# Both feed-forward products of a hybrid encoder step as Strassen block products on one Trainium2 core

## The chip, the cores and the metric

The kernel runs on one core of a Trainium2 chip (trn2). The metric is device time in microseconds (us): how long one execution takes on that core. Engines are named as in the profile: PE is TensorE (matmuls; PEld its weight loads), DVE is VectorE, ACT is ScalarE, POOL is GpSimd, SP is SyncE, whose queue issues most DMAs.

## The reference

One step of a one-layer encoder for 512 prompt tokens and 64 sample tokens, 576 in all, with D_MODEL 2048 and D_FF 5632, in float32. The token mixer (sliding-window attention, a state-space branch, cross-attention into 256 memory tokens, three gates) comes first. The change concerns what follows it:

```
def conv_ffn(h, conv_prev, lp):
    t = h.shape[1]
    up = h @ lp['w_up']                       # 2048 -> 2 x 5632
    a, bv = jnp.split(up, 2, axis=-1)
    a_ext = jnp.concatenate([conv_prev.astype(a.dtype), a], axis=1)
    conv_w = lp['conv_w']
    a_conv = sum(a_ext[:, i:i + t] * conv_w[i] for i in range(CONV_W)) + lp['conv_b']
    out = (jax.nn.gelu(a_conv) * bv) @ lp['w_down']   # 5632 -> 2048
    return out, a_ext[:, -(CONV_W - 1):]

def layer(x, attn_past, s0, conv_prev, mem_k, mem_v, table, lp):
    ...
    x = x + rms_norm(mix, lp['norm_post_mix'])
    h2 = rms_norm(x, lp['norm_pre_ffn'])
    f, conv_new = conv_ffn(h2, conv_prev, lp)
    x = x + rms_norm(f, lp['norm_post_ffn'])
```

## The kernel before

**Layout.** Activations are kept transposed: channels on the 128 partitions, the 576 tokens along the row, in two halves of 288 (HT). A product's output row tile is 128 channels x 576 tokens in two PSUM banks.

**Three passes.** Float32 products are made of fp32r matmuls: each operand is split into a high part (rounded to fp32r) and a low part (what is left), and `gemm` (line 154) adds three products, high x high, high x low and low x high. A k-tile of 128 thus costs 3 passes x 2 halves = 6 matmuls of 288 columns per row tile, each with its own weight load.

**Weight stream.** The program is a list of blocks (`block`, line 91); a block is one weight tile of up to 128 x 1024 and a function that uses it. `go(i)` (line 1718) runs block i, and ahead of it issues the DMA of block i + 5 into one of four `raw` buffers (SP's queue, `dma_to`), makes the high part of block i + 2 on ScalarE (`h_to`, line 107, tile `wh`) and the low part of block i + 1 (of i + 2 for short blocks and at the end) on VectorE (`l_to`, line 118, tile `wl`); three buffers each. Each engine carries out its instructions in the order in which the program issues them; semaphores between the engines come from the tiles that they share.

**Side work** that isn't tied to a block is a list of generators (`side`); `side_step` advances one of them by a step between k-tiles.

**Feed-forward.** `up1_run` (line 1386) makes the first four row tiles of a k-tile by k-tile while x1, the residual after the mixer, is still being finished (`x1_next`); x1 also goes to DRAM (`x1d`). `ffn_open` then lays out the tiles of this phase, and `ffn_sums` and `ffn_rbc` make the norm's scale per token, which is applied to the outputs (`rbc`). Four tiles of the second half of w_up follow (`up_tile(i, 1)`), and for each further i a tile of each half: 40 x 2 tiles, each of 16 k-tiles in two blocks. `up_run` (line 1478) evicts a tile of the first half by a multiplication on VectorE (line 1497) and does the conv, GELU and scale (`conv`, line 1457: three VectorE instructions of 576 columns, one activation, one GpSimd multiplication at line 1475); a tile of the second half is multiplied with it (line 1503) and split into `gh` and `gl` (lines 1504, 1505), which stay on the chip. After every four of these tiles `down_run` (line 1517) takes their four k-tiles of w_down through all 16 output tiles, 8 blocks, and adds the result to `f` in SBUF (line 1529). The last four k-tiles are done by `last_run` (line 1532) in two parts of the tokens, with the second norm and residual behind each (`tail_*`). `x1tok` transposes x1 into token rows for that residual, as side work.

## Time and profile before

| | us |
|---|---|
| median of 3 runs | 3061.28 (3060.11 to 3063.08) |
| span of the profiled execution | 3060.8 |
| first matmul of the tail (line 1546) in that execution, from the span's start | 2978.34 |

The profiled execution has no other time beside its span; it lies 0.5 us below the median. The page gives the busy time of each engine, the span in slices, the chain of work that ended last, and the costliest groups of instructions, each with its line, what it writes and reads, the count, its busy time, the mean of one in ns and the idle time before. The 5504 x 3 matmuls on `xh` and `xl` at line 159 are those of the input and output projections and of up; the 1280 x 3 on `gh` and `gl` are down's. The blocks outside the feed-forward and the tail issue the same instructions after the change.

### The profile page before, as it was taken

How to read it: one execution, taken by the hardware profiler on the slowest of the kernel's cores; microseconds unless marked ns; L12 is line 12 of the kernel's file. 1: busy time of each engine (PE TensorE's matmuls, PEld its weight loads, DVE VectorE, ACT ScalarE, POOL GpSimd, SP SyncE). 2: the span in 40 equal slices, each digit the busy share in tenths (PEclk: the TensorE clock that was granted, in tenths of full speed). 3: DMA queues.
4: the chain of work that ended last, by engine and by line, in shares of the span. 5: the costliest groups of instructions: out<-in, count | busy, mean ns of one | idle time of the engine just before them, and what ended most of it. 6: DMA issues, size and time to landing. Idle time of an engine off the chain costs nothing.

```text
span 3060.8 us, 52554 instructions
## 1 busy us (share of the span) xinstructions
PE 3019.4 (99%) x22827; PEld 2964.2 (97%) x22827; DVE 1317.8 (43%) x2065; ACT 803.9 (26%) x1120; POOL 510.1 (17%) x548
## 2 busy tenths in 40 slices
PE   8999999999999999989999999999999999999997
PEld 7999999999999999979999999999999999999997
DVE  7334532444432243495444444434343434343447
ACT  4323332222222244452111212121212121212123
POOL 2200010133330024372020201010101010101015
PEclk9999999999999999999999999999999999999999
DMA  8622342334333345653333333222222222222235
GB/s 273 186 80 64 92 120 86 107 108 112 104 99 106 97 139 153 195 189 99 95 114 91 114 89 97 83 83 83 83 83 83 82 84 81 83 82 83 81 98 195
DMA packets 478630, 334.80 MB, mean 109 GB/s; under 512 B 57916, under 2 KB 447218, under 8 KB 477056
## 3 DMA queue, kind: packets, MB, share of 16 engines
q1 hardware_dynamic: 467344, 299.99, 33.1%
q0 software_dynamic: 6320, 21.99, 2.3%
q10 hardware_dynamic: 4736, 9.47, 0.8%
q8 instruction: 179, 2.93, 0.4%
q14 instruction: 51, 0.42, 0.0%
HBM read 293.22 MB, written 38.89 MB: 109 GB/s over the span
## 4 chain that ended last, share of the span: by engine, by line
PE 94%; DVE 3%; DMA 1%; POOL 1%; issue 1%; ACT 0%; DVEq 0%; ACTq 0%; POOLq 0%
PE ps L159 87%; PE ps L181 2%; PE ps L284 1%; DVE wl L118 1%; PE ps L1546 1%; DVE xl L1357 1%; DMA raw<-in_w_mem_kv_dram 0%; PE ps L1027 0%; PE ps L1031 0%; PE ps L579 0%; PE ps L613 0%; DMA raw<-in_w_out_dram 0%; PE ps L691 0%; POOL mixq L1347 0%; PE ps L662 0%
## 5 line engine op out<-in xcount | busy, mean ns | idle before, releaser
L159 PE MATMUL ps<-xh,wh 128*128 128x288 f32 x5504 | 1200.8, 298 | 3.1 <-DVE r_ss L1323 2.0
L159 PE MATMUL ps<-xh,wl 128*128 128x288 f32 x5504 | 1190.9, 296 | 7.6 <-DVE wl L118 7.6
L159 PE MATMUL ps<-xl,wh 128*128 128x288 f32 x5504 | 1189.6, 296 | 3.2 <-DVE xl L1357 3.2
L159 PEld LDWEIGHTS ps<-xh,wh 128*128 128x128 f32 x5504 | 889.0, 189 | 15.8 <-issue 9.9
L159 PEld LDWEIGHTS ps<-xh,wl 128*128 128x128 f32 x5504 | 890.6, 189 | 9.8 <-DVE wl L118 9.7
L159 PEld LDWEIGHTS ps<-xl,wh 128*128 128x128 f32 x5504 | 890.3, 189 | 4.7 <-DVE xl L1357 4.6
L107 ACT CAST wh<-raw 128x1024 fp32r<-128x1024 f32 (+2 forms) x478 | 482.1, 1009 | 992.3 <-PE ps L159 717.4
L118 DVE TENSOR_TENSOR wl<-raw,wh 128x1024 fp32r<-128x1024 f32 (+2 forms) x486 | 597.1, 1237 | 232.4 <-ACT wh L107 232.1
L159 PE MATMUL ps<-gh,wh 128*128 128x288 f32 x1280 | 274.2, 296 | 0.0
L159 PE MATMUL ps<-gl,wh 128*128 128x288 f32 x1280 | 274.1, 296 | 0.0
L159 PE MATMUL ps<-gh,wl 128*128 128x288 f32 x1280 | 274.0, 296 | 0.0
L1529 DVE TENSOR_TENSOR f<-ps,f 128x576 f32<-128x576 f32 x144 | 109.1, 758 | 243.5 <-PE ps L159 240.9
L159 PEld LDWEIGHTS ps<-gh,wl 128*128 128x128 f32 x1280 | 206.2, 189 | 0.0
L159 PEld LDWEIGHTS ps<-gl,wh 128*128 128x128 f32 x1280 | 206.2, 189 | 0.0
L159 PEld LDWEIGHTS ps<-gh,wh 128*128 128x128 f32 x1280 | 206.2, 189 | 0.0
L1461 POOL COPY cst<-mtmp 128x2 f32<-128x2 f32 x43 | 8.3, 193 | 1064.7 <-DVE mtmp L1497 1054.1
L1497 DVE TENSOR_TENSOR mtmp<-ps,rbc 128x576 f32<-128x576 f32 x40 | 30.3, 758 | 311.4 <-PE ps L159 311.4
L1503 DVE TENSOR_TENSOR c<-ps,c 128x576 f32<-128x576 f32 x44 | 33.3, 757 | 275.5 <-PE ps L159 269.8
L1474 ACT ACTIVATE c<-c,cvt 128x576 f32<-128x576 f32 x44 | 34.2, 778 | 390.9 <-DVE c L1473 390.9
L1143 ACT COPY ev<-ps 128x576 f32<-128x576 f32 x48 | 30.8, 642 | 272.9 <-PE ps L159 272.9
L1504 ACT CAST gh<-c 128x576 fp32r<-128x576 f32 x44 | 29.7, 674 | 271.4 <-DVE c L1503 271.4
L1475 POOL TENSOR_TENSOR c<-c,rbc 128x576 f32<-128x576 f32 x44 | 71.1, 1615 | 103.6 <-ACT c L1474 103.6
(407 smaller groups left out, 2009.7 us busy)
## 6 DMA issues: line engine op xcount, KB each, us to landing
raw<-in_w_up_dram SPq DMA_DIRECT2D x180, 512.0 KB
raw<-in_w_in_dram SPq DMA_DIRECT2D x118, 512.0 KB
raw<-in_w_down_dram SPq DMA_DIRECT2D x96, 512.0 KB
gd<-ev SPq DMA_DIRECT2D x48, 288.0 KB
gate<-gd SPq DMA_DIRECT2D x48, 288.0 KB
raw<-in_w_mem_kv_dram SPq DMA_DIRECT2D x16, 512.0 KB
raw<-in_w_out_dram SPq DMA_DIRECT2D x72, 96.0 KB
raw<-in_w_out_dram SPq DMA_DIRECT2D x18, 384.0 KB
```

Source lines behind the costliest of these rows:

```text
L107: (nc.vector.tensor_copy if 4 <= i < KD else nc.scalar.copy)(h[:, 0:n], raws[i][:, 0:n])
L118: E.tensor_tensor(out=lo[:, 0:n], in0=raw[:, 0:n], in1=hls[i][0][:, 0:n].bitcast(F32), op=ALU.subtract)
L159: mm(ps[:, a, 0:HT], w[:, c0:c0 + P], x[:, a * HT:(a + 1) * HT], start=start and i == 0, stop=stop and i == 2,)
L181: nc.tensor.transpose(out, in_, ident[0:k, 0:k])
L284: mm(mps[t][:, a, :], x[:, c], w[:, a * 512:(a + 1) * 512], start=k == 0 and i == 0, stop=k == KD - 1 and i == 2)
L1143: nc.scalar.copy(halves(e), ps[:, :, 0:HT])
L1357: nc.vector.scalar_tensor_tensor(out=xl[:, k, c], in0=x1[:, c], scalar=gcol[:, G_FFN, k:k + 1], in1=xh[:, k, c].bitcast(F32), op0=ALU.mult ...
L1474: nc.scalar.activation(c, c, AF.Gelu_apprx_tanh, bias=w(3))
L1475: nc.gpsimd.tensor_tensor(out=c, in0=c, in1=F["rbc"], op=ALU.mult)
L1503: nc.vector.tensor_tensor(out=halves(c), in0=ps[:, :, 0:HT], in1=halves(c), op=ALU.mult)
L1529: nc.vector.tensor_tensor(out=halves(f), in0=ps[j][:, :, 0:HT], in1=halves(f), op=ALU.add)
L1546: mm(ps[:, j, 0:n], w[:, c], x, start=k == 0 and i == 0, stop=k == 3 and i == 2)
```

## The change

Each pair of row tiles (up: A11, A12, A21, A22 are the two row tiles by the two halves of the k-tiles; down: two output tiles by k-tiles taken in twos) with the two halves of the tokens is a 2 x 2 block product. It is made in seven block products (Strassen's scheme in Winograd's order) in place of eight. Four of the seven weight operands of a group are sums that VectorE makes from weight tiles before they are split as any other (`s_to`); the activations' operands are made once:

- up: `xcombos` reads x1 back from DRAM k-tile by k-tile, makes the four combined operands on GpSimd and VectorE, splits them, and puts three of them into a new tile E; the fourth goes through DRAM (`x4d`) and, by `x4_load`, into the place of a plain operand that isn't needed any more. The first four tiles of each half of w_up stay as before.
- between: the conv's steps run as side work (`conv_pair`, `conv_steps`), its first multiplication on ScalarE, its scaling and the product with the second half on GpSimd. `gcombos` makes and splits the seven operands for down and stores them to DRAM (`gcd`), on ScalarE's queue (high parts) and GpSimd's (low parts).
- down: runs after all of up, in five chunks of 8 k-tiles (4 pairs), each chunk for 8 pairs of output tiles. `ring_load` brings a chunk's seven operands from DRAM through GpSimd's queue, the first chunk's one by one behind the products of the last up group, into two sets of slots in the space of xh, xl and E. The last 4 k-tiles stay plain (`last_run`, which takes its operands from the same slots).

A group's products go to three PSUM banks (A, C, A, B, A, C, A); a bank is copied out and added to again. x1's transposition (`xtok`) has its copies on ScalarE now. There are 3 `raw` buffers in the shared pool and one or two extra ones in a phase's own pool. In the diff's core, `stt` is a VectorE SCALAR_TENSOR_TENSOR, and context lines are cut.

```diff
+    def raw_tile(kind):
+        if extra["pool"] is not None and extra["kind"] == kind:
+            extra["turn"] = (extra["turn"] + 1) % (3 + extra["n"])
+            if extra["turn"] >= 3:
+                return extra["pool"].tile([P, 1024], F32, tag="rawx", name="raw", bufs=extra["n"])
+        return wp.tile([P, 1024], F32, tag="raw", name="raw", bufs=3)
...
+    def s_to(j):
+        while pos["s"] <= min(j, len(blocks) - 1):
+            i = pos["s"]
+            n, src = blocks[i][0], blocks[i][3]
+            raws[i] = src() if src else raws[i][:, 0:n]
+            pos["s"] += 1
...
+            lo = w_tile("wl", kind)
+            out, hi = as_src(raw, lo, n), as_src(raw, hls[i][0], n).bitcast(F32)
+            if kind == 2:
+                nc.vector.scalar_tensor_tensor(
+                    out=out, in0=raw, scalar=1.0, in1=hi, op0=ALU.mult, op1=ALU.subtract
+                )
+            else:
+                E = nc.gpsimd if i >= len(blocks) - 8 and i % 2 else nc.vector
+                E.tensor_tensor(out=out, in0=raw, in1=hi, op=ALU.subtract)
...
                 kk = kb * 2 + k
-                if kk == KD - 1:
-                    ffn_open()
                 x1_next()
...
+                if kk == KD - 1:
+                    ffn_open()
+                    for j in range(NG1):
                         (nc.vector.tensor_copy if j % 2 else nc.scalar.copy)(
-                            halves(F["a"][j][:, 2:2 + T]), ps[:, :, 0:HT])
+                            halves(F["a"][j][:, 2:2 + T]), F["ps"][j][:, :, 0:HT])
                         if j == 1:
                             ffn_sums()
...
+    def opnd(o, hl, s0, n=None):
+        x = (xh_t, xl_t)[hl][0]
+        ps = lambda k: k if n is None else slice(k, k + n)
+        if o in (0, 3):
+            return x[:, ps(s0), HT:T] if o else x[:, ps(s0), 0:HT]
+        if o in (1, 2):
+            return x[:, ps(8 + s0), 0:HT] if o == 1 else x[:, ps(8 + s0), HT:T]
+        return F["E"][:, hl, (2, 0, 1)[o - 4], ps(s0), :]
+    SEVEN = (0, 5, 4, 1, 6, 2, 3)
+    def product(bank, h, lo, j, n, s0, start, hook=None):
+        o = SEVEN[j]
+        for p in range(n):
+            xh, xl = opnd(o, 0, s0 + p), opnd(o, 1, s0 + p)
+            for i, (w, x) in enumerate(((h, xh), (h, xl), (lo, xh))):
+                mm(bank, w[:, p * P:(p + 1) * P], x, start=start and p == 0 and i == 0, stop=p == n - 1 and i == 2,
+                   skip_group_check=True)
+            if hook:
+                hook(p)
...
+    def stt(out, a, s, b, op):
+        nc.vector.scalar_tensor_tensor(out=out, in0=a, scalar=s, in1=b, op0=ALU.mult, op1=op)
+    def low(out, x, hi):
+        stt(out, x, 1.0, hi.bitcast(F32), ALU.subtract)
...
+    def xcombos():
+        E = F["E"]
+        G = nc.gpsimd
+        for p in range(8):
+            xa, xb = x_bufs(p)
+            a0, a1, b0, b1 = xa[:, 0:HT], xa[:, HT:T], xb[:, 0:HT], xb[:, HT:T]
+            for x, k in ((xa, p), (xb, p + 8)):
+                G.tensor_scalar(out=x, in0=x, scalar1=gcol[:, G_FFN, k:k + 1], scalar2=None, op0=ALU.mult)
+            G.tensor_tensor(out=a0, in0=a0, in1=a1, op=ALU.subtract)
+            G.tensor_tensor(out=a1, in0=b1, in1=a1, op=ALU.subtract)
+            yield
+            yield
+            yield
+            stt(b1, a0, -1.0, b1, ALU.subtract)
+            stt(b0, b1, -1.0, b0, ALU.subtract)
+            x2 = xa.rearrange("p (o c) -> p o c", o=2)
+            nc.scalar.copy(E[:, 0, 0:2, p, :], x2)
+            yield
+            nc.scalar.copy(E[:, 0, 2, p, :], b1)
+            gh = F["p"].tile([P, T], F32R, tag="gh", name="gh", bufs=2)
+            nc.scalar.copy(gh[:, 0:HT], b0)
+            low(E[:, 1, 0:2, p, :], x2, E[:, 0, 0:2, p, :])
+            nc.scalar.dma_start(x4d[0, :, p], gh[:, 0:HT].bitcast(F32))
+            yield
+            gl = F["p"].tile([P, T], F32R, tag="gl", name="gl")
+            low(E[:, 1, 2, p, :], b1, E[:, 0, 2, p, :])
+            low(gl[:, 0:HT], b0, gh[:, 0:HT])
+            nc.gpsimd.dma_start(x4d[1, :, p], gl[:, 0:HT].bitcast(F32))
+            if p + 2 < 8:
+                x_load(p + 2)
+    def x4_load():
+        for hl in range(2):
+            nc.gpsimd.dma_start(opnd(3, hl, 0, 8).bitcast(F32), x4d[hl])
...
+    def conv_steps(i, a):
         cv = cvt
         w = lambda j: cv[:, j, i:i + 1]
+        c = ev("c")
+        F["c", i] = c
+        e = F["p"].tile([P, 6], F32, tag="e", name="e", bufs=2)
+        nc.scalar.activation(c, a[:, 2:578], AF.Identity, scale=w(2))
+        nc.gpsimd.tensor_copy(e[:, 0:2], cv[:, 4:6, i])
+        nc.gpsimd.tensor_copy(e[:, 2:4], a[:, 514:516])
...
+        yield
...
-        V.tensor_scalar(out=c, in0=a[:, 2:578], scalar1=w(2), scalar2=None, op0=ALU.mult)
         V.scalar_tensor_tensor(out=c, in0=a[:, 1:577], scalar=w(1), in1=c, op0=ALU.mult, op1=ALU.add)
         V.scalar_tensor_tensor(out=c, in0=a[:, 0:576], scalar=w(0), in1=c, op0=ALU.mult, op1=ALU.add)
+        yield
...
+        yield
...
+    def scaled(a):
+        nc.gpsimd.tensor_tensor(out=a[:, 2:2 + T], in0=a[:, 2:2 + T], in1=F["rbc"], op=ALU.mult)
...
+    def conv_pair(q):
+        yield
+        yield
+        g0, g1 = (conv_steps(2 * q + m, F["a2"][m]) for m in range(2))
+        for g in (g0, g0, g0, g1, g0, g1, g0, g1, g1, g1):
+            next(g, None)
+            yield
...
+    def g_out(x, gh, ops, q, n=T):
+        gl = F["p"].tile([P, T], F32R, tag="gl", name="gl")
+        low(gl[:, 0:n], x[:, 0:n], gh[:, 0:n])
+        store(0, ops, q, gh)
+        store(1, ops, q, gl)
...
+    def gcombos(q):
+        c0, c1 = F.pop(("c", 2 * q)), F.pop(("c", 2 * q + 1))
+        plain = q >= NI // 2 - N_PLAIN
+        n = T if plain else HT
+        gh0 = g_hi(c0, n)
+        yield
...
+        a0, a1, b0, b1 = c0[:, 0:HT], c0[:, HT:T], c1[:, 0:HT], c1[:, HT:T]
+        nc.gpsimd.tensor_tensor(out=a0, in0=a0, in1=a1, op=ALU.subtract)
+        nc.gpsimd.tensor_tensor(out=a1, in0=b1, in1=a1, op=ALU.subtract)
+        for _ in range(3):
+            yield
+        g_out(c1, gh1, (1, 2), q)
+        yield
+        stt(b1, a0, -1.0, b1, ALU.subtract)
+        stt(b0, b1, -1.0, b0, ALU.subtract)
+        gh0 = g_hi(c0)
+        yield
+        gh1 = g_hi(c1)
+        yield
+        yield
+        g_out(c0, gh0, (5, 6), q)
+        for _ in range(4):
+            yield
+        g_out(c1, gh1, (3, 4), q)
...
+    def up2_run(i, kb):
...
+                side_step()
...
+                c = F["c", i]
+                nc.vector.tensor_tensor(out=halves(c), in0=ps[:, :, 0:HT], in1=halves(c), op=ALU.mult)
+                if i % 2 == 1:
+                    side.insert(0, gcombos(i // 2))
+            elif i == NG1 - 1:
+                side_drain()
+                x4_load()
...
+    def up_group(q, part):
+        R = {}
+        last = q == NI // 2 - 1 and part == 1
...
+                    F["sum"] = F["p"].tile([P, 4 * 578], F32, tag="sa", name="sums")
+                s = [F["sum"][:, 0:1024], F["sum"][:, 1024:2048]]
+                g = lambda x: s[x] if isinstance(x, int) else R[x]
+                stt(s[j], g(a), 1.0, g(b), ALU.add)
+                return s[j]
...
+        def run(j):
+            def run_(h, lo):
...
+                s1, s5, s2 = S["s"]
+                bank = (A, C, A, B, A, C, A)[j]
+                product(bank, h, lo, j, 8, 0, j in (0, 1, 3), lambda p: side_step() if p % 2 else None)
+                d0, d1 = F["a2"]
+                lo_, hi_ = slice(2, 2 + HT), slice(2 + HT, 2 + T)
+                if j == 0:
+                    nc.scalar.copy(s1, A)
+                elif j == 1:
+                    nc.scalar.copy(s5, C)
+                elif j == 2:
+                    nc.scalar.copy(s2, A)
+                elif j == 3:
+                    nc.vector.tensor_tensor(out=d0[:, lo_], in0=B, in1=s1, op=ALU.add)
+                elif j == 4:
+                    stt(d1[:, hi_], A, -1.0, s5, ALU.subtract)
+                elif j == 5:
+                    nc.vector.tensor_tensor(out=d0[:, hi_], in0=C, in1=s2, op=ALU.add)
+                    after(0)
                 else:
...
+                    nc.scalar.activation(d1[:, lo_], A, AF.Identity, scale=-1.0)
+                    after(1)
+                    if not part:
+                        side.append(conv_pair(q))
+                    elif not last:
+                        side.append(gcombos(q))
...
+                if last:
+                    ring_load(0, SEVEN[j])
...
+                    if j == 6:
+                        down_open()
...
+        def after(m):
+            a = F["a2"][m]
+            if not part:
+                scaled(a)
+                return
+            c = F["c", 2 * q + m]
+            E = nc.vector if last else nc.gpsimd
+            E.tensor_tensor(out=c, in0=c, in1=a[:, 2:2 + T], op=ALU.mult)
+        srcs = [lambda: R["A11"], add(0, "A21", "A22"), add(1, 0, "A11"), lambda: R["A12"],
+                add(0, "A11", "A21"), add(1, 1, "A12"), lambda: R["A22"]]
+        loads = [ld("A11", 0, 0), both, None, ld("A12", 0, 1), None, None, None]
+        for j in range(7):
+            block(1024, loads[j], run(j), srcs[j], 2)
...
+    def ring_load(c, o):
+        n = NP if c < NCH else N_PLAIN
+        for hl in range(2):
+            nc.gpsimd.dma_start(opnd(o, hl, 4 * (c % 2), n).bitcast(F32), gcd[hl, o, :, c * NP:c * NP + n, :])
...
+    def down_open():
+        side_drain()
+        for _ in gcombos(NI // 2 - 1):
+            pass
...
+        for o in SEVEN:
+            ring_load(1, o)
...
+    def down_group(c, mp):
...
+                    R["sum", j] = sum_tile(j)
...
+                nc.vector.tensor_tensor(out=o.rearrange("p (j c) -> p j c", j=NP), in0=v(a), in1=v(b), op=ALU.add)
...
+        srcs = [lambda: blk(0, 0), add(0, (1, 0), (1, 1), True), add(1, 0, (0, 0), True), lambda: blk(0, 1),
+                add(2, (0, 0), (1, 0), True), add(1, 1, (0, 1), False), lambda: blk(1, 1)]
...
+                bank = (A, C, A, B, A, C, A)[j]
+                product(bank, h, lo, j, NP, 4 * (c % 2), j in (0, 1, 3))
+                f0, f1 = F["f"][2 * mp], F["f"][2 * mp + 1]
+                f11, f12, f21, f22 = f0[:, 0:HT], f0[:, HT:T], f1[:, 0:HT], f1[:, HT:T]
+                dst = (f11, f22, f12, f11, f22, f12, f21)[j]
+                plus = j not in (1, 4, 6)
+                if c == 0 and j in (0, 1, 2, 6):
+                    nc.scalar.activation(dst, bank, AF.Identity, scale=1.0 if plus else -1.0)
+                else:
+                    nc.vector.tensor_tensor(out=dst, in0=dst, in1=bank, op=ALU.add if plus else ALU.subtract)
+                if mp == 0 and j == 6 and c >= 1:
+                    for o in SEVEN if c + 1 < NCH else (0, 3, 1, 2):
+                        ring_load(c + 1, o)
+            return run_
+        for j in range(7):
+            block(512, load if j == 0 else None, run(j), srcs[j], 3)
...
+        et = F["ep"].tile([P, 2 * 3 * 8 * HT], F32, tag="E", name="et")
+        F["ft"], F["grow"], F["acc"] = et[:, 0:10240], et[:, 10240:12288], et[:, 12288:12288 + T]
+        g = I["norm_post_ffn"]
+        nc.gpsimd.dma_start(F["grow"], bass.AP(g.tensor, g.offset, [[0, P], [1, D]]))
...
     def go(i):
-        dma_to(i + RAW_AHEAD)
-        h_to(i + 2)
-        l_to(i + (2 if N_SHORT <= i < LATE0 or i >= len(blocks) - 8 else 1))
+        if i < N_U2 + 8:
+            dma_to(i + RAW_AHEAD)
+            h_to(i + 2)
+            l_to(i + (2 if N_SHORT <= i < LATE0 else 1))
+        elif i < N_DOWN:
+            dma_to(min(i + 9, N_DOWN))
+            s_to(i + 3)
+            h_to(i + 2)
+            l_to(i + 2)
+        elif i < N_TAIL:
+            last = N_TAIL - 1 if i < N_TAIL - 2 else N_TAIL
+            dma_to(i + 8)
+            s_to(min(i + 4, last))
+            h_to(min(i + 3, last))
+            l_to(min(i + 3, last))
+        else:
+            dma_to(i + 4)
+            h_to(i + 2)
+            l_to(i + (2 if i >= len(blocks) - 8 else 1))
```

The blocks are listed in the order: the first four tiles of the first half of w_up, those of the second, the 40 groups of up, the 40 of down, the tail.

More of the change, by code (lines that the diff above doesn't have):

```diff
@@ L1430, in ffn_rbc @@
     def ffn_rbc():
-        ps = ps_rot()
+        ps = ps_side()
         bcast_cols(ps, F["y"])
@@ L1450, in ffn_open @@
-        F["cst"] = p.tile([P, 2, 2, NI], F32, name="cst")
-    def first_conv(j):
-        a = F["a"][j]
-        nc.vector.tensor_tensor(out=a[:, 2:2 + T], in0=a[:, 2:2 + T], in1=F["rbc"], op=ALU.mult)
-        conv(j, a)
-    def conv(i, a):
+        extra.update(pool=p, n=2, kind=2, turn=0)
+        F["xr"] = [p.tile([P, 1024], F32, tag="rawx", name="xc", bufs=2) for _ in range(2)]
+        sa = p.tile([P, 4 * 578], F32, tag="sa", name="a4")
+        F["a"] = [sa[:, j * 578:(j + 1) * 578] for j in range(4)]
@@ L1557, in run @@
                 l_to(cur["i"] + 2)
-            if a == 1 and mb == 0:
-                for hf in range(2):
-                    F["xs", hf] = wp.tile([P, 1024], F32, tag="raw", name="xs", bufs=4)
-                    nc.sync.dma_start(F["xs", hf][0:64], x1td[512:576, hf * 1024:(hf + 1) * 1024])
             if a == 1 and 1 <= mb <= 6:
```

358 lines of the change are left out of this document (224 added, 134 removed).

## The prediction

> **What bounds the kernel now.** I read the page first, then the chain that ended last in order of time, then the busy times of the feed-forward stretch, then the single instructions that the change multiplies. From the page:
>
> ```profile
> span 3060.8 us, 52554 instructions
> PE 3019.4 (99%) x22827; PEld 2964.2 (97%) x22827; DVE 1317.8 (43%) x2065; ACT 803.9 (26%) x1120; POOL 510.1 (17%) x548
> PE 94%; DVE 3%; DMA 1%; POOL 1%; issue 1%; ACT 0%; DVEq 0%; ACTq 0%; POOLq 0%
> ```
>
> TensorE is the chain. Busy time of pipelined matmuls doesn't say how fast they follow each other; the chain in order of time does (start, length, what):
>
> ```profile
> 1851.97 1126.40 PE ps L159 x8448
> 2985.81 3.52 PE ps L1546 x24
> ```
>
> 8448 matmuls of 288 columns without a break in 1126.40 us: 133.3 ns each. The second row is the tail, whose matmuls have 320 columns and go three times running into one PSUM bank: 146.7 ns each, that is 32 columns more at the same 13 ns over the columns at 2.4 per ns. So running into one bank costs nothing, and I price the new products, 24 or 12 matmuls into one bank, at 133.3 ns.
>
> The other engines in the same stretch (busy us of PE, weight load, DVE, ACT, POOL, then granted clock, DMA share, GB/s):
>
> ```profile
> 1600.00:2954.00 1354.00, 1354.00 (x10164) 1354.00 (x10164) 543.17 (x684) 263.81 (x280) 119.89 (x198) 1.00 0.29 86
> ```
>
> VectorE is busy 40%, ScalarE 19%, GpSimd 9%, DMA 29%. The room that the change must fit in is VectorE's other 60%.
>
> **What goes.** Up: 40 groups (20 pairs of row tiles in each half of w_up) take 2 x 96 matmuls each before, 7 products x 8 x 3 = 168 after: 7680 to 6720. Down: 10 chunks x 8 x 48 = 3840 to 5 x 8 x 7 x 4 x 3 = 3360. 1440 matmuls fewer at 133.3 ns: **-192.0 us**. The rest of the program's matmuls stay, the 80 transposes of x1 too; only their evictions move, from VectorE to ScalarE, which has the time (below).
>
> **What comes, on VectorE and GpSimd.** One instruction at a time: first VectorE, then GpSimd.
>
> ```profile
> 2007.17 0.76 DVE L1505 TENSOR_TENSOR gl<-c,gh 128x576 fp32r<-128x576 f32 x1 [0.74 <-ACT gh L1504]
> 2007.85 2.36 DVE L118 TENSOR_TENSOR wl<-raw,wh 128x1024 fp32r<-128x1024 f32 x2
> 2020.61 0.82 DVE L1470 SCALAR_TENSOR_TENSOR c<-mtmp,cvt,c 128x576 f32<-128x576 f32 x1
> 2021.86 0.22 DVE L1473 SCALAR_TENSOR_TENSOR c<-e,cvt 128x2 f32<-128x2 f32 x1
> 2022.00 1.22 DVE L118 TENSOR_TENSOR wl<-raw,wh 128x1024 fp32r<-128x1024 f32 x1
> L1265 DVE TENSOR_TENSOR gate<-ps,gate 128x288 f32<-128x288 f32 x8 | 3.6, 449 | 0.0
> L118 DVE TENSOR_TENSOR wl<-raw,wh 128x512 fp32r<-128x512 f32 x17 | 11.6, 681 | 0.0
> ```
>
> ```profile
> 1325.05 0.90 POOL L1348 TENSOR_TENSOR mixq<-mixq,xTr 128x288 f32<-128x288 f32 x1
> 1408.71 1.43 POOL L1475 TENSOR_TENSOR c<-c,rbc 128x576 f32<-128x576 f32 x1 [2.36 <-ACT c L1474]
> L1008 POOL MEMSET tz<- 128x1024 f32 x6 | 5.7, 956 | 33.3 <-PE ps L959 26.2 <-DMA tz<-kt 3.7 <-PE ps L1031 3.5
> ```
>
> A SCALAR_TENSOR_TENSOR is 0.06 us dearer than a TENSOR_TENSOR (0.82 against 0.76), so 1.28 for 1024 columns; an instruction behind another starts about 0.08 early (2.36 for two of 1.22), so 1.20 in a row, and in the same way 0.43 for 288 columns (0.82 less 288 columns at 1.03 ns, the slope between 0.76 and 1.22).
>
> Take a pair of up tiles, both halves of w_up, as the unit. TensorE: 336 x 133.3 = 44.8 us (51.2 before). VectorE: 14 low parts and 8 sums of 1024 columns, 22 x 1.20 = 26.4; two convs, each 2 x 0.82 + 3 x 0.22, with gaps 4.7; the combinations of the products' operands (gcombos), 3 of 288 and 3 of 576 columns, 3.7 with the 0.08 taken off; 6 evictions from PSUM at 0.45, 2.7. Together **37.5 us, 84%** of TensorE's 44.8. ScalarE, whose rows are
>
> ```profile
> L107 ACT CAST wh<-raw 128x1024 fp32r<-128x1024 f32 x410 | 429.5, 1047 | 903.4 <-PE ps L159 641.8 <-issue 222.3 <-ACT wh L107 27.5
> L1143 ACT COPY ev<-ps 128x576 f32<-128x576 f32 x48 | 30.8, 642 | 272.9 <-PE ps L159 272.9
> ```
>
> has 14 casts, 14.7 us, 8 small evictions of about 0.4 and some 8 others of 0.4 to 0.8: 24 us, half its time. It is hidden. So are the transfers: four weight tiles, 2.1 MB, per 22.4 us and 2.1 MB of stores per 44.8 us are 94 and 46 GB/s, on DMA engines that are busy 29% at 86; if they were late, each late weight tile would cost TensorE its delay, as the buffers hold five tiles.
>
> GpSimd gets 6 TENSOR_TENSOR of 576 columns and 2 of 288 per pair, 10.4 us, besides small copies and DMA issues. By itself that is nothing in 44.8. But the two engines shut each other out:
>
> ```profile
> 1553.02 0.80 POOL L1465 COPY e<-mtmp 128x2 f32<-128x2 f32 x1
> 1556.18 2.32 POOL L1475 TENSOR_TENSOR c<-c,rbc 128x576 f32<-128x576 f32 x1 [2.36 <-ACT c L1474]
> 1559.81 0.58 POOL L1600 DMA_DIRECT2D xr<-x1d  x1
> ```
>
> ```profile
> 1552.95 0.82 DVE L1469 SCALAR_TENSOR_TENSOR c<-mtmp,cvt,c 128x576 f32<-128x576 f32 x1
> 1553.81 0.82 DVE L1470 SCALAR_TENSOR_TENSOR c<-mtmp,cvt,c 128x576 f32<-128x576 f32 x1
> 1555.99 3.59 DVE L118 TENSOR_TENSOR wl<-raw,wh 128x1024 fp32r<-128x1024 f32 x2
> ```
>
> GpSimd's multiplication starts inside the first of two low parts and takes 2.32 instead of 1.43; the two low parts take 3.59 instead of 2.36. So VectorE pays 1.23 for one GpSimd multiplication of 576 columns, nearly all of it, and I put 0.7 for one of 288. It pays nothing for GpSimd's small copies (0.82 and 0.82 beside the 0.80). Per pair 6 x 1.23 + 2 x 0.7 = 8.8, so VectorE needs 37.5 + 8.8 = 46.3 if every one hits. Its PSUM evictions and two-column instructions (4.0 of the 37.5) can run beside GpSimd; that saves about a ninth of the 8.8, which leaves 45.3. Both stand above 44.8, and VectorE also waits for casts and products now and then, with two products (6.4 us) of lookahead to absorb it. I take **46.2 per pair, +1.4 over TensorE, x 20 = +28 us**. Ends: 0 (all of it absorbed) and 49.7 per pair (46.3 and another 3.4 us of waits in VectorE's order of work), +98.
>
> The Trainium skill says the same in "SBUF — State Buffer", section "SBUF: two separate sides": VectorE with two SBUF inputs and a GpSimd instruction that reads SBUF hold a shared port pair exclusively, for a whole instruction. It speaks against this change, which loads both; with whole instructions, 37.5 + 10.4 = 47.9, this term would be 62 us. The trace agrees in kind, with 1.23 of the 1.43 as the price.
>
> **Opening of the up products.** While the four remaining plain tiles run (384 matmuls, 51.2 us), xcombos builds the x operands. VectorE: 8 low parts at 1.14, 9.1; eight k-tile pairs of 4 x 0.43 + 0.74, 19.7; four convs 9.2; one gcombos 3.7; evictions and the rest 4: 45.7. GpSimd's shut-outs: 16 scalings of 576 columns, not in the trace, between 0.5 (the memset's rate, 956 ns for 1024) and 1.23: I take 0.7, 11; 18 of 288 at 0.7, 12.6; 8 of 576 at 1.23, 9.8: 33.4. Together 79, less some 4 beside PSUM work, against 51.2. VectorE runs in order, so its backlog holds the low parts behind it, and TensorE with them: **+24 us**. Ends 8 (scalings beside VectorE, lookahead used up) and 38 (1.23 each). The reload of the last of these operands (x4_load) waits on GpSimd's queue for their stores and for half of the fourth plain tile; behind it stand the first up group's scalings, which nobody wants for another 20 us. The eviction of the four accumulators now stands behind all of the last k-tile instead of between: +1.
>
> **Down.** A group is 84 matmuls, 11.2 us. VectorE: 11 of 512 columns at 0.60 in a row and 7 evictions at 0.45, 9.8 us; GpSimd only issues loads. That fits, 88%, with a bank's next product one product (1.6 us) away: 0. Without that cover, 0.1 us per product would be 28 us over 280.
>
> Its operands come from DRAM: 1.18 MB for each of seven, issued one product (3.2 us) apart in the last up group.
>
> ```profile
> q0 software_dynamic: 6320, 21.99, 2.3%
> ```
>
> 21.99 MB in 2.3% of the span are 312 GB/s; weights take 2.1 MB per 22.4 us, 94, which leaves 218 or 5.4 us an operand. Each load waits on GpSimd's queue for its product; what stands behind it there is the next load and the last stores, since the last group's multiplications are VectorE's. From that group's start the sixth lands at 35.6 and the seventh at 41.0, where the down products want them at 30.4 and 32.0. The weights pause when TensorE does: **+8 us**, ends 0 and 15. Later chunks have 90 us for 8.3 MB and stay hidden. The tail gets three weight buffers for four and loads its norm weights late: +3, ends 0 and 10.
>
> **Sum** against the profiled span, 3060.8, 0.5 below the median of the runs: 3060.8 - 192.0 + 28 + 24 + 1 + 8 + 3 = 2932.8; for the median **2933 us**.
>
> **Rivals.** First, the shut-out is absorbed: up pairs run at 44.8 and the opening at its low end: 3061.3 - 192 + 8 + 1 + 4 + 3 = 2885. For it: VectorE's 45.3 is only 1% over. Against: the opening needs half as much again as there is time for.
>
> Second, VectorE's order of work costs more than its sum: a conv step that waits for a late GpSimd product holds every low part behind it. At 49.7 per pair, 2933 + 70 = 3003. For it: GpSimd's 1.43 became 2.32 with VectorE busy 40%, and it is to be 84%.
>
> Third, slower than before: if all that GpSimd does at the port shuts VectorE out, its small copies (3.2 us per pair) and DMA issues (stores and row loads, about 10 of 0.6) too, a pair is 37.5 + 10.4 + 3.2 + 6 = 57.1, +12.3 x 20 = 246, so 3061.3 - 192 + 246 + 36 = 3151. It decides from (192 - 36) / 20 + 44.8 = 52.6 per pair. Against: the 0.82 beside the 0.80 copy. The box on DMAs from GpSimd's queue in the same section of the skill has descriptors starve while VectorE runs in a two-port mode; the only two-port work left here is small, and the row of 0.58 stands in a stretch in which VectorE was busy.
>
> That the change doesn't do what it says is no rival for the count: 1440 is fixed by the loops. For the pace it would be, and the 146.7 ns speak against it.
>
> **Chances.** Forecast (2905 to 2965) 0.54; absorbed (2875 to 2905) 0.17; order of work (2965 to 3050) 0.20; slower 0.08; no difference 0.01. The range of 2885 to 3000 takes the first whole, some 0.13 of the second and of the third each: 0.80. 0.2%, 6 us, is about what a measurement here tells from no change: faster 0.91, same 0.01, slower 0.08.
>
> **What would show it.** Right: 1440 fewer matmuls; a product of 24 at 3.2 us where nothing stalls; up pairs of some 46 us, TensorE waiting there for wl, and VectorE's 1024-column instructions with a mean well above 1.28; the longest waits between the plain tiles and the first up products; a short wait for DMA at the first down group, and down groups at 11.2. Wrong: up pairs at 44.8 (absorbed) or 49 (order of work), a down group over 11.2, or products slower than 133.3 ns a matmul with nothing awaited.

## The result, and the profile after

The changed kernel takes **3349.9 us** (median of 4 runs, 3349.0 to 3352.5) against 3061.8 for the kernel before (3060.1 to 3063.1): a ratio of 1.094, 95% interval 1.093 to 1.096. The forecast was 2933 us, faster; it is 9% slower. The profiled execution spans 3347.5 us, 415 more than the forecast's 2932.8.

The page of the changed kernel, the span, the busy times and the chain by engine:

```profile
span 3347.5 us, 52463 instructions
PE 2958.1 (88%) x21387; PEld 2831.3 (85%) x21387; DVE 1888.4 (56%) x2875; ACT 1140.9 (34%) x1772; POOL 903.5 (27%) x897
PE 71%; DVE 14%; DMA 5%; issue 4%; ACT 3%; POOL 2%; ACTq 0%; DVEq 0%; SPq 0%; POOLq 0%
```

The 1440 matmuls are gone (22827 to 21387), and TensorE is still most of the chain. But it is busy 88% instead of 99%, and no other engine is full. So this is waiting, and the next question is where. The busy times by stretch, one in the up products and one in the down products (PE, weight load, DVE, ACT, POOL, then granted clock, DMA share, GB/s):

```profile
2054.00:2334.00 280.00, 240.05 (x1681) 231.30 (x1681) 200.94 (x221) 110.09 (x153) 103.09 (x101) 0.97 0.39 113
2890.00:3017.00 127.00, 100.82 (x681) 94.17 (x681) 78.34 (x147) 33.12 (x56) 9.23 (x14) 0.96 0.40 135
```

VectorE is busy 72% and 62% here. If it or GpSimd were the bound, it would be near full. The waits of TensorE's matmuls in the up groups, for what, how long in all, how often, and the longest:

```profile
PE ps L1528 <- ACT s L1778: 81.0, 39, 6.1
PE ps L1528 <- DVE a L1534: 32.1, 39, 1.8
PE ps L1528 <- DVE a L1786: 24.4, 38, 0.6
PE ps L1528 <- ACT s L1776: 19.6, 40, 0.5
```

Four waits, each 38 to 40 times, in 40 groups: once per group each. Every one is for an eviction of A or C (L1776 reads A after the first product, L1778 C after the second, L1534 A after the fifth, L1786 C after the sixth). None is for a weight. The down groups show the same with nothing around it; these are TensorE's rows with a wait in one round of seven products, from the sixth of one group to the sixth of the next, and the evictions on VectorE that end the first four:

```profile
2952.92 0.37 PE L1528 MATMUL ps<-xh,wh 128*128 128x288 f32 x1 [0.64 <-DVE f L1907]
2955.39 0.38 PE L1528 MATMUL ps<-xh,wh 128*128 128x288 f32 x1 [0.64 <-DVE f L1907]
2959.45 0.50 PE L1528 MATMUL ps<-E,wh 128*128 128x288 f32 x2 [0.64 <-DVE f L1907]
2961.92 0.50 PE L1528 MATMUL ps<-E,wh 128*128 128x288 f32 x2 [0.64 <-ACT wh L149]
2967.56 0.37 PE L1528 MATMUL ps<-xh,wh 128*128 128x288 f32 x1 [0.64 <-DVE f L1907]
```

```profile
2952.32 0.46 DVE L1907 TENSOR_TENSOR f<-f,ps 128x288 f32<-128x288 f32 x1
2954.79 0.45 DVE L1907 TENSOR_TENSOR f<-f,ps 128x288 f32<-128x288 f32 x1 [0.81 <-PE ps L1528]
2958.85 0.45 DVE L1907 TENSOR_TENSOR f<-f,ps 128x288 f32<-128x288 f32 x1
2961.32 0.46 DVE L1907 TENSOR_TENSOR f<-f,ps 128x288 f32<-128x288 f32 x1 [0.81 <-PE ps L1528]
```

VectorE starts an eviction, and 0.60 us later TensorE starts the next product, four times in a group of 14.64 us (2952.92 to 2967.56). (The row that names ScalarE's cast starts at the same 0.60; the profile puts a wait down to the last event ahead of it.) A wait costs more than the 0.64 us of idle time in its row: 14.64 is 3.44 over the 11.2 of the matmuls, 0.86 for each of the four, because matmuls that follow each other every 0.13 us overlap (a row lasts some 0.3), and the overlap ends and starts again. The product that waits is never one into the accumulator being evicted: after A comes C, after C comes A. By its data it has to wait for nothing. The one thing that A and C share is their PSUM tile: they are its two halves. Where the next product goes into B, which lies in another tile, or into A after B, TensorE runs through.

### The profile page after: what moved, and what is told of

Same layout as the page of the kernel before. It is cut to its first block, busy times and chain, and to the rows that moved or that the text cites. A ratio compares the mean times of both kernels' runs of the same rounds, so it can differ in the third digit from the quotient of the medians.

```text
span 3347.5 us, 52463 instructions
## 1 busy us (share of the span) xinstructions
PE 2958.1 (88%) x21387; PEld 2831.3 (85%) x21387; DVE 1888.4 (56%) x2875; ACT 1140.9 (34%) x1772; POOL 903.5 (27%) x897
## 4 chain that ended last, share of the span: by engine, by line
PE 71%; DVE 14%; DMA 5%; issue 4%; ACT 3%; POOL 2%; ACTq 0%; DVEq 0%; SPq 0%; POOLq 0%
PE ps L205 33%; PE ps L1528 33%; DVE wl L166 2%; DMA gcd<-gl 2%; DMA raw<-in_w_down_dram 2%; DVE wl L161 2%; DVE f L1907 2%; PE ps L230 2%; ACT wh L149 2%; DVE ws L1883 1%; PE ps L333 1%; DVE sums L1534 1%; DVE gl L1534 1%; DVE xl L1406 1%; DVE a L1534 1%
## 5 line engine op out<-in xcount | busy, mean ns | idle before, releaser
L1528 PE MATMUL ps<-E,wh 128*128 128x288 f32 x2880 | 618.7, 308 | 155.8 <-ACT s L1778 82.5
L1528 PEld LDWEIGHTS ps<-E,wh 128*128 128x128 f32 x2880 | 477.2, 195 | 191.3 <-ACT s L1778 91.9
L149 ACT CAST wh<-raw 128x1024 fp32r<-128x1024 f32 (+2 forms) x481 | 431.8, 900 | 488.7 <-PE ps L205 290.4
L166 DVE TENSOR_TENSOR wl<-raw,wh 128x1024 fp32r<-128x1024 f32 (+2 forms) x369 | 380.5, 1032 | 251.1 <-ACT wh L149 248.0
L1528 PE MATMUL ps<-E,wl 128*128 128x288 f32 x1440 | 435.1, 302 | 0.0
L161 DVE SCALAR_TENSOR_TENSOR wl<-sums,wh 128x1024 fp32r<-128x1024 f32 x160 | 245.2, 1532 | 181.7 <-ACT wh L149 181.7
L1528 PEld LDWEIGHTS ps<-E,wl 128*128 128x128 f32 x1440 | 281.8, 196 | 0.0
L149 ACT CAST wh<-ws 128x512 fp32r<-128x512 f32 x157 | 97.3, 619 | 372.2 <-DVE ws L1883 372.2
L149 ACT CAST wh<-sums 128x1024 fp32r<-128x1024 f32 x160 | 167.5, 1047 | 135.5 <-PE ps L1528 127.4
L1907 DVE TENSOR_TENSOR f<-f,ps 128x288 f32<-128x288 f32 x248 | 112.6, 454 | 177.9 <-PE ps L1528 177.9
```

The costliest lines, as they stand in the source:

```text
L149: (nc.vector.tensor_copy if 4 <= i < KD else nc.scalar.copy)(as_src(raws[i], h, n), raws[i])
L161: nc.vector.scalar_tensor_tensor(out=out, in0=raw, scalar=1.0, in1=hi, op0=ALU.mult, op1=ALU.subtract)
L166: E.tensor_tensor(out=out, in0=raw, in1=hi, op=ALU.subtract)
L1528: mm(bank, w[:, p * P:(p + 1) * P], x, start=start and p == 0 and i == 0, stop=p == n - 1 and i == 2, skip_group_check=True)
L1907: nc.vector.tensor_tensor(out=dst, in0=dst, in1=bank, op=ALU.add if plus else ALU.subtract)
```

## The experiments

Theory: the program orders a matmul into one half of the tile behind the eviction of the other half. The rival to begin with is the prediction's own, that VectorE with GpSimd's shut-outs is the bound. Gains are differences of medians. Line numbers shift by a few between kernels.

**e1: a tile of its own for A, B and C.**

```diff
+    ROT = ((0, 1, 2), (3, 2, 1))
+
+    def tiles3():
+        S["g"] += 1
+        return [ps_at(k) for k in ROT[S["g"] % 2]]
...
-                    S["g"] += 1
-                    t = 2 * (S["g"] % 2)
-                    x, y = ps_at(t), ps_at(t + 1)
-                    S["A"], S["C"], S["B"] = x[:, 0, 0:HT], x[:, 1, 0:HT], y[:, 0, 0:HT]
+                    x, z, y = tiles3()
+                    S["A"], S["C"], S["B"] = x[:, 0, 0:HT], z[:, 0, 0:HT], y[:, 0, 0:HT]
```

> The three accumulators A, B and C of a group each lie in a PSUM tile of their own (in the changed kernel A and C are the halves of one tile). Shared-tile theory: TensorE's waits ahead of the second, third, sixth and seventh product of a group are there only because the program orders a matmul into one half of the tile behind the eviction of the other half. Then they go: a down group falls from 14.65 us to about 11.2 (four waits of 0.86), 40 x 3.4 = 138 us; in the up groups the 157 us of these waits and 34 us of restarting go in part, as VectorE is next (pairs from 55.5 to between 46 and 50), 110 to 190 us. Total 3020 to 3100 us. Rival, VectorE with GpSimd's shut-outs is the bound: the waits turn into waits for low parts, up pairs stay at 53 or more, down groups at 13 or more, total above 3230 us.

Measured: 3112.8 us (3107.9 to 3118.8), 237 less than the changed kernel, ratio to before 1.017 (1.015 to 1.018). A down group takes 11.2 us, the forecast's figure, in all but the first two of each chunk. The up pairs (here and below the mean of the 19 distances between the first evictions of every other group) fall from 56.5 to 50.9 us. That is below the rival's 53 and just above the theory's 50; the total is 13 us above the theory's range and 117 below the rival's. What the matmuls of the up groups wait for now:

```profile
PE ps L1528 <- ACT s L1784: 43.4, 19, 3.2
PE ps L230 <- DMA xtok<-x1d: 22.6, 8, 3.8
PE ps L230 <- ACT xtok L1724: 2.3, 1, 2.3
PE ps L1528 <- DVE a L1534: 1.8, 5, 0.8
```

Of the four waits none is left but five short ones. Two new rows stand in their place, one per pair of groups, and both are taken up below.

**e2: the dose.** A and B are the halves of one tile, C is alone.

```diff
-                    S["A"], S["C"], S["B"] = x[:, 0, 0:HT], x[:, 1, 0:HT], y[:, 0, 0:HT]
+                    S["A"], S["B"], S["C"] = x[:, 0, 0:HT], x[:, 1, 0:HT], y[:, 0, 0:HT]
```

> A dose of the same: A and B are the halves of one tile, C is alone. By the shared-tile theory two products of a group (the fourth and the fifth) have to wait for the eviction of the other half instead of four, so about half of what the kernel with three tiles gains is gained: 130 to 170 us, total 3180 to 3230, with TensorE's waits ahead of products 4 and 5 and none ahead of 2, 3, 6 and 7. Rival, the waits are of the bank that is evicted itself or of VectorE's order of work: waits stay ahead of 2, 3, 6 and 7, total within 60 us of the changed kernel's 3350.

Measured: 3316.3 us (3308.3 to 3321.3), only 34 less than the changed kernel, far from the 130 to 170 expected. In the down groups the dose is exact: 12.9 us against 14.6 with four waits and 11.2 with none. In the up groups the waits moved as the theory says, to the fourth product (for A's eviction, L1780) and the fifth (for B's, L1782), with none left at the other places:

```profile
PE ps L1528 <- ACT s L1780: 94.6, 29, 4.7
PE ps L1528 <- DVE a L1782: 53.5, 37, 4.3
```

But these two cost as much as the four before, and pairs take 59.0 us instead of 56.5. So the waits follow from which accumulators share a tile, and a count of them is not their price. (In all these kernels the halves of a tile are also neighbours in PSUM, and no run separates the two. For the tile speaks that in the profile the waits of the up groups end with a semaphore of the engine that evicts, so they are waits that the program asks for.) The wait for L1780 is up to 4.7 us long: that is the eviction of the third product, which is late in e1 as well (L1784 there, 3.2), where only the fifth product needs it.

**e3 and e7: the operands' loads.** The distances between e1's down groups are 17.2 us in the first chunk's opening, 20.4, 20.0 and 19.8 at the start of the next three, 14.8 at the start of the last, and 11.2 to 12.5 in between. e3 asks for one operand per group instead of all behind the chunk's first group; e7 does the same through SyncE's queue, on e4, from the first chunk on (the second chunk's loads leave the code that opens the down products). This is e7's edit; e3's keeps `c >= 1` and GpSimd's queue.

```diff
-                if mp == 0 and j == 6 and c >= 1:
-                    for o in SEVEN if c + 1 < NCH else (0, 3, 1, 2):
-                        ring_load(c + 1, o)
+                if j == 6:
+                    ops = SEVEN if c + 1 < NCH else (0, 3, 1, 2)
+                    if mp < len(ops):
+                        ring_load(c + 1, ops[mp], nc.sync)
```

> Three tiles as in e1, and the next chunk's seven operands are loaded one per down group instead of all fourteen transfers behind the chunk's first group. Theory, the burst of 8.3 MB delays the weights' transfers behind it, and that is the 8 to 16 us wait for w_down in every chunk: the waits go from five chunks, 35 to 60 us less than e1. Rival, the waits are for the weights alone (their buffers come free late): within 8 us of e1.

> e4 with the next chunk's operands loaded through SyncE's queue, one operand per down group, so that they stand between the weights' transfers; in e3 they still left in one burst, since GpSimd's queue ran ahead of the groups (14 transfers between 2610.9 and 2625.6 us). Burst theory: the long gaps at the start of each chunk (5.5 and 8.5 us at the first, 7.2 to 7.8 at the next three, 2.7 at the last) go, 40 to 65 us less than e4. Rival, the weights are late at a chunk's start for a reason of their own: within 10 us of e4.

e3: 3107.7 us, 5 less than e1. It didn't do what it says: GpSimd's queue, ahead of the groups, waits only until TensorE is through with the operand's last reader, and issues. The first and last of the loads for one chunk in e3, in the timeline of GpSimd:

```profile
2610.90 0.75 POOL L1843 DMA_DIRECT2D xh<-gcd  x1 [75.79 <-PE ps L1528]
...
2625.61 0.75 POOL L1843 DMA_DIRECT2D xl<-gcd  x1 [1.29 <-DMA E<-gcd]
```

While they run, the DMA engines are busy 97% and move 337 GB/s (the last two figures):

```profile
2610.00:2630.00 20.00, 19.74 (x149) 19.50 (x147) 12.96 (x23) 7.73 (x15) 9.28 (x14) 1.00 0.97 337
```

e7: 3042.5 us (3039.9 to 3054.5), 51 less than e4, as the burst theory says. On SyncE's queue a load is issued behind the weights' transfers that were asked for before it. All 39 distances between down groups are 11.2 us, and TensorE doesn't stop in 420:

```profile
2510.00:2930.00 420.00, 419.65 (x3159) 419.44 (x3158) 349.05 (x649) 162.20 (x292) 0.00 (x0) 1.00 0.57 180
```

The DMA engines are busy 57% and move 180 GB/s. With the 97% of e3 this says that the 8.3 MB at once made the weights late. e7 changed the queue and the pace together, though, and no run paced the loads on GpSimd's queue, so the queue's own share isn't separated.

**e4 and e12: the opening of the up products.** e4 scales the rows of x on ScalarE (on e1); e12 issues the next k-tile's scalings (on ScalarE) and subtractions (on GpSimd) ahead of this one's store and loads in GpSimd's queue (on e11).

```diff
-                G.tensor_scalar(out=x, in0=x, scalar1=gcol[:, G_FFN, k:k + 1], scalar2=None, op0=ALU.mult)
+                nc.scalar.activation(x, x, AF.Copy, scale=gcol[:, G_FFN, k:k + 1])
```

> Three tiles as in e1, and the sixteen scalings of 576 columns in the opening of the up products run on ScalarE instead of GpSimd. Theory, GpSimd's own time (two scalings of 1.72, two subtractions of 0.8, a transfer pair of 1.1 per k-tile) is what TensorE waits for in the opening, 57 us of gaps there: 25 to 35 us less than e1. Rival, VectorE's backlog is what it waits for: within 10 us of e1.

> e11, and in the opening the next k-tile's scaling and subtractions go ahead of this one's store and load in GpSimd's queue. Theory: the gaps of the opening (12.2, 3.5, 5.2, 2.5, 3.3, 8.5 us in e8) are a chain from VectorE's low part through GpSimd's store, its next row loads and its subtractions back to VectorE; without it 10 to 20 us less than e11. Rival, VectorE's own backlog is what is late (54 us of work in 102): within 6 us of e11.

TensorE's waits from 1378 us to the first product's start, in the changed kernel and in e4:

```profile
PE ps L205 <- DVE wl L166: 43.7, 5, 18.7
PE ps L1528 <- DVE wl L161: 12.0, 1, 12.0
```

```profile
PE ps L205 <- DVE wl L166: 25.6, 5, 11.9
PE ps L1528 <- DVE wl L161: 8.3, 1, 8.3
```

e4: 3093.5 us, 19 less than e1, between the two expectations, with 34 us of waits for 56. One scaling took GpSimd 1.72 us:

```profile
L1554 POOL TENSOR_SCALAR a<-a,gcol x8: 1712/1724/1736, 1380.7 to 1458.5; 128x576 f32<-128x576 f32 x8
```

e12: 2930.0 us, 1.6 less than e11, so that theory falls: the chain through GpSimd's store and loads isn't what the rest of the opening waits for; 28 us stay. The rival, VectorE's own backlog, has the time right, but VectorE is busy only 60 of the 102 us from 1378 in e12. A part is known from e10 (below), which leaves out GpSimd's multiplications by `rbc` here too: TensorE's waits are 23.5 us there and 33.4 in e8, and VectorE's waits for ScalarE's first step of a conv, which follows such a multiplication, 2.5 and 11.7. What the others wait for was not separated.

**e5 and e6: the two rows that e1 left in the up groups.** In e1, ScalarE's queue at one of the 19 long waits, and behind it TensorE's row:

```profile
2200.99 1.05 ACT L149 CAST wh<-sums 128x1024 fp32r<-128x1024 f32 x1
2205.76 0.78 ACT L1604 ACTIVATE c<-c,cvt 128x576 f32<-128x576 f32 x1 [3.73 <-DVE c L1602]
2206.45 0.38 ACT L1784 COPY s<-ps 128x288 f32<-128x288 f32 x1
```

```profile
2206.88 0.53 PE L1528 MATMUL ps<-E,wh 128*128 128x288 f32 x2 [3.15 <-ACT s L1784]
```

The gelu (L1604) waits 3.73 us for three instructions of two columns on VectorE, which stand behind sums and low parts there. The eviction of the third product stands behind the gelu, and TensorE behind the eviction. e5 moves the gelus back. e6 issues the row load for the x1 transposes a product earlier and gives the transposes the fourth tile instead of B's other half. Both are made on e4.

```diff
-        for g in (g0, g0, g0, g1, g0, g1, g0, g1, g1, g1):
-            next(g, None)
+        for g in (g0, g0, g0, g1, g1, g1, None, None, None, g0, g1, g0, g1):
+            if g:
+                next(g, None)
             yield
```

```diff
-                if 2 <= gi < 2 + KD:
+                if 2 <= gi < 2 + KD and j:
                     xtok(gi - 2, j, S["spare"])
+                if 1 <= gi < 1 + KD and j == 6:
+                    xtok(gi - 1, 0, None)
```

> e4 with the two gelus of a pair moved back by about one product in the order of the side steps. In e1 and e4 TensorE stands 3.45 us once per pair ahead of the fifth product (18 to 19 of the 20 pairs, or 1.35 to 2.45 where it has stood already), because ScalarE's eviction of the third product's accumulator is queued behind a gelu that waits for VectorE's two-column instructions. Order-of-work theory (the second rival of the prediction): the stall goes, and with it the dip of the granted clock behind it (216 matmuls take 30.2 us after it instead of 28.8); pairs from 50 to 46 to 47.5 where no x1 transposes run, 50 to 80 us less than e4 in all. Rival, VectorE's sum of work is the bound: the stall moves to another place, within 20 us of e4.

> e4 with the row load of x1 for the transposes issued one product earlier (at the end of the group before) and the transposes' PSUM bank in the fourth tile instead of beside B. Theory: the eight waits of TensorE for this load (2.5 to 4 us each, one per pair in the first eight pairs) and their clock dips go, 25 to 40 us less than e4. Rival: they only shift the stall behind the gelu (1.35 us there, 3.45 elsewhere) back to its full size: 5 to 12 us less.

e5: 3036.3 us (3033.4 to 3040.8), 57 less than e4, as the order-of-work theory has it; pairs without transposes 45.9 to 47.4. This is the order of work, not its sum: nothing was taken off VectorE. e6: 3069.3 us (3062.4 to 3074.4), 24 less, just under the theory's range; the waits for the transposes' loads are gone, and a part came back as waits for the late eviction (52.7 us for it instead of 41.5).

**e8: all three edits on e4.**

> The three edits of e5, e6 and e7 together on e4. If they are independent, the gains add: 115 to 185 us less than e4, 2910 to 2980 us, the forecast of 2933 inside. Rival, VectorE with GpSimd's shut-outs is the next bound: up pairs stay at 48.5 or more and the total above 3000 us.

Measured: 2974.9 us (2974.0 to 2979.8), ratio to before 0.972 (0.970 to 0.973): 119 less than e4, at the low end of the expected 115 to 185, where the three alone add up to 132. Pairs take 47.3 us on average, below the rival's 48.5.

**e9 and e10: the shut-outs between GpSimd and VectorE.** Both leave out the multiplications by the reciprocal rms of x1, 4 of GpSimd's 6 per pair, so the feed-forward input isn't normalized; e9 in the changed kernel, e10 in e8.

```diff
-        nc.gpsimd.tensor_tensor(out=c, in0=c, in1=F["rbc"], op=ALU.mult)
...
-        nc.gpsimd.tensor_tensor(out=a[:, 2:2 + T], in0=a[:, 2:2 + T], in1=F["rbc"], op=ALU.mult)
+        pass
```

> The changed kernel itself (A and C in one tile), with four of GpSimd's six multiplications of 576 columns per pair left out: those by the reciprocal rms of x1, for the value and the gate rows of w_up and in the first four tiles, so that the feed-forward input stays unnormalized. Shared-tile theory: VectorE has room for the shut-outs as long as TensorE waits for evictions; 10 to 50 us less than 3350, pairs still above 53. Rival (the third of the prediction, GpSimd shuts VectorE out with all it does, and that is what made the change slow): pairs below 51, 110 us less or more.

> The same multiplications left out of e8, whose pairs take 47.3 us against 44.8 for TensorE's matmuls alone. If the shut-outs are the rest (VectorE is busy 819 of 960 us there, 3.4 us per pair above the 37.5 of its own sum), pairs fall to 45.0 to 46.0, 25 to 45 us less than e8. Rival, the rest is waits in VectorE's order, for the landing of the low halves' stores (74.5 us in 45 waits in e8): within 12 us of e8.

e9: 3325.1 us, 25 less than the changed kernel, pairs 55.9 on average. Its four waits are still there:

```profile
PE ps L1528 <- ACT s L1777: 75.2, 38, 6.0
PE ps L1528 <- DVE a L1534: 26.3, 39, 1.7
PE ps L1528 <- DVE a L1785: 23.8, 37, 0.6
PE ps L1528 <- ACT s L1775: 18.6, 38, 0.5
```

The prediction's third rival had the sign right, and its mechanism isn't what made the change slow. e10: 2925.1 us, 50 less than e8 (25 to 45 were expected; the opening, where the same multiplications go, has 10 less of waits), pairs 45.4: where TensorE no longer waits for evictions, the shut-outs do count.

**e11: the low halves' single buffer.** e8 with two of a pair's four low halves written over their own source.

```diff
-        gl = F["p"].tile([P, T], F32R, tag="gl", name="gl")
+        gl = x.bitcast(F32R) if own else F["p"].tile([P, T], F32R, tag="gl", name="gl")
```

> e8, where the last two of the four low halves of a pair are written over their own source instead of into the single buffer that the store before must have left. If VectorE's waits for those stores (74.5 us in 45 waits) are what is left of the pairs' 2.5 us over TensorE, the waits fall to a third and the time by 15 to 40 us. Rival, VectorE catches them up in its 15% of room: within 8 us of e8.

Measured: **2931.6 us** (2929.4 to 2935.6), ratio to before 0.958 (0.956 to 0.959), 43 less than e8, a little more than the expected 15 to 40. Pairs without transposes take 45.0 us, 0.2 over TensorE's 44.8. VectorE's waits for the store's landing in the up groups, in e8, e10 and e11:

```profile
DVE gl L1534 <- DMA gcd<-gl: 74.5, 45, 9.8
```

```profile
DVE gl L1534 <- DMA gcd<-gl: 68.7, 47, 6.6
```

```profile
DVE gl L1534 <- DMA gcd<-gl: 27.3, 20, 9.7
```

e10 keeps the waits and loses the shut-outs, e11 keeps the shut-outs and loses most of the waits, and both bring the pairs to about 45.4. So neither alone is "the rest"; VectorE seems to have had room for one of the two, but not for both. The price of a shut-out follows from VectorE's busy time in the up stretch of e8, e10 and e11:

```profile
1480.00:2440.00 960.00, 920.04 (x6824) 911.82 (x6823) 818.70 (x887) 451.41 (x636) 459.49 (x462) 0.99 0.51 150
```

```profile
1480.00:2400.00 920.00, 909.25 (x6824) 905.82 (x6823) 749.23 (x892) 451.15 (x638) 298.36 (x378) 1.00 0.53 155
```

```profile
1480.00:2400.00 920.00, 907.77 (x6798) 903.37 (x6798) 802.42 (x885) 448.90 (x635) 439.95 (x459) 0.99 0.53 155
```

e8 is the same kernel as e10 but for the multiplications: 818.7 us in 20.3 pairs of 47.3 against 749.2 in 20.3 of 45.4 are 3.4 us a pair, 0.84 for each of the four. e11, whose pairs are as long as e10's, has 53.2 us more than e10, 2.6 a pair, 0.66 each. So a shut-out costs 0.66 to 0.84 us on average.

## Why the prediction was wrong

The changed kernel's 415 us over the forecast, by place (profiled executions; distances between instructions in the trace):

| part | forecast | measured | difference |
|---|---|---|---|
| opening: TensorE's waits for low parts | 24 | 56 | +32 |
| up pairs, 20 | 46.2 each | 56.5 each | +206 |
| down groups, 40 | 11.2 each | 14.6 each | +136 |
| first groups of the later chunks, over 14.6 | 0 | 7.4, 8.6, 7.5, 0.5 | +24 |
| tail, from its first matmul | +3 (82.5 before) | 88.6 | +3 |
| the rest, most of it around the first down group | 9 | 23 | +14 |

**The step that failed** is the line on the down groups, "That fits, 88%, with a bank's next product one product (1.6 us) away: 0", and the same thought behind the up groups, where the evictions from PSUM were priced as VectorE's time only. It took the bank for the unit of the dependence. In the program it is the tile: after A comes C, in the same tile, and no product lies between an eviction and the next matmul into that tile. The prediction gave a price for having no cover, 0.1 us per product for 28 us over 280; it was 3.4 us per group of seven, 0.49 per product, 136 us, and e1's groups have none of it. In the up pairs e1 took away 5.6 of the 10.3 us too many. As a whole the down products got 119 us shorter in e1 (595.4 to 476.8 between the first and the last group's last eviction; the chunk starts took back some of the 136) and the up pairs 112, nearly all of its 237. The waits cost more than the 192 us that the products save. The Trainium skill, in "PSUM — Partial Sum Buffer", section "Summary: rules for kernel authors", has a reader of PSUM kept apart from a running matmul by bank; A and C, 512 float32 columns apart, lie in two banks by the page's 512 float32 values a bank. The kernel waited all the same, 0.64 us each time in the down groups: a rule of the chip is a lower bound on the waits, and the program may order more.

**Matmuls, -192.** Right: 1440 fewer, and 3159 in 419.65 us (e7) are 132.8 ns each, for the 133.3 assumed. Products into one bank run at full pace.

**Up pairs, 46.2.** The sum for VectorE was too high: 200.9 us in 280 are 40.5 per pair in the changed kernel, 802.4 in 920 are 39.6 in e11, all in, where 37.5 + 8.8 = 46.3 were forecast. VectorE's own work was about right (37.0 in e10, without four of the six multiplications). One shut-out costs 0.66 to 0.84 us, not the 1.23 of the single case that was read as typical. The first rival, "absorbed", has the right end: 45.0 in e11. But VectorE's order of work did matter once the tile waits were gone, as the second rival had it in kind: 50.9 in e1, of which the late gelu (e5) was 2.7. In detail it is another case. The rival had VectorE stand behind a late GpSimd product, and the low parts behind VectorE; in e1 ScalarE stands behind VectorE's queue, and an eviction behind ScalarE. The transposes' load (1.4, e6) was nowhere in the prediction, which said that ScalarE "has the time" for their evictions: it has, but not its queue.

**Opening, +24.** Wrong in size, 56, and in kind. The prediction took VectorE's backlog for the limit, 75 us of work against 51.2. In the changed kernel VectorE is busy less than half of the time there and stands idle for GpSimd's subtractions (`a` and `xc` are buffers of the k-tiles in turn):

```profile
1378.00:1480.00 102.00, 57.83 (x377) 56.32 (x377) 44.92 (x80) 25.44 (x41) 62.61 (x75) 0.78 0.40 122
```

```profile
DVE a L1534 <- POOL a L1556: 15.5, 2, 8.3
DVE xc L1534 <- POOL xc L1556: 12.4, 2, 7.1
```

The scalings stand ahead of the subtractions in GpSimd's queue, and one takes 1.72 us and not the 0.7 that was taken from a memset; the upper end, 38, assumed 1.23. With the scalings on ScalarE (e4) 34 of the 56 remain, still 10 over the forecast.

**Ring loads, +8 and "stay hidden".** The first part was on the low side; the second is wrong. 8.3 MB have 90 us by the bytes, but GpSimd issued them within some 15 us (e3's rows), and the weights came late. e7 shows the same bytes hidden when they are paced.

**Third rival.** 0.08 for slower was the chance for GpSimd's shut-outs at twice their size. e9 excludes it: 25 us, where it would have been 110 or more. The rival that happened, a wait of TensorE for its own evictions, wasn't among them, although the chain of products into A, C, A, B, A, C, A was in the diff and each of its places could have been priced.

What stays open: what most of the remaining 28 us of the opening wait for, how the chunk starts divide between the burst and the queue, and why the two waits of e2's up groups cost as much as four. That the late eviction, which e2's fourth product needs without a product of cover, is the reason is argued from its waits, and no run separated it.

## What to carry to other kernels

When a change makes accumulators shorter-lived, follow each one from its last matmul to its eviction to the next matmul into *any part of the same tile*, and price that gap per product: 0.86 us, of which 0.60 from an eviction's start to the next matmul, four times in a group, made 3.4 us on 11.2. This change took matmuls away and put work into in-order queues, so look for the instruction behind which an eviction or a load stands, not only for the sum of an engine. And a result against the forecast needn't condemn the idea: with its tiles apart, its loads paced, the scalings on ScalarE, two orderings mended and two low halves written in place, the same seven products take 4.2% off the kernel before.

## What the runs showed of the hardware

The granted clock falls to half behind most of TensorE's longer stalls. In e1, ten-microsecond stretches behind two of the waits for the late eviction, and the stretch after the second:

```profile
2060.00:2070.00 10.00, 10.00 (x77) 10.00 (x76) 9.11 (x9) 4.06 (x6) 2.86 (x2) 1.00 0.41 107
2207.00:2217.00 10.00, 10.00 (x64) 10.00 (x65) 7.46 (x9) 3.82 (x4) 2.35 (x2) 0.83 0.19 56
2217.00:2227.00 10.00, 10.00 (x78) 10.00 (x77) 8.61 (x9) 4.63 (x8) 5.82 (x6) 1.00 0.50 146
```

The first stretch follows a wait of the same length as the second (3.18 and 3.15 us) and shows nothing; the second has 64 matmuls for 78, 1.8 us lost on top of the stall. The profile has the clock at 0.50 from 2208.0 to 2211.4, and at 1.00 before and after. A shorter stall can be enough:

```profile
1593.01 0.53 PE L1528 MATMUL ps<-E,wh 128*128 128x288 f32 x2 [1.84 <-ACT s L1784]
```

```profile
1594.00:1604.00 10.00, 10.00 (x67) 9.97 (x66) 8.16 (x9) 3.79 (x5) 3.04 (x4) 0.85 0.27 80
```

By the clock that the profile records, 18 of the 22 stalls of 1.84 to 3.8 us in e1's up groups were followed by such a stretch, mostly of 3.4 us; and none of the seven of 0.8 to 1.1 us. Short waits don't do it: the changed kernel's down groups with four of 0.64 run at 1.00 in a stretch without a chunk's start.

```profile
2950.00:2980.00 30.00, 24.89 (x176) 23.25 (x175) 19.52 (x37) 8.28 (x14) 0.00 (x0) 1.00 0.23 71
```

The Trainium skill, in "TensorE: Matmul & The Clock Gate", section "What's actually happening", has half the clock after an idle window of about 3.4 us that runs freely, and full clock after a busy one. The half clock, its 3.4 us and the stall that went unpunished agree with it. That a stall of 1.84 us was enough doesn't: it is well short of the page's idle window, and the measurement decides.
